# A fifth tile for the running block sums, and another spread of the partner steps, in a decoder layer on one core

## The chip, the core and the metric

The kernel runs on one core of a Trainium2 chip. The metric is the device time of one execution in microseconds; of several runs the median counts. The profile is that of one execution, taken by the hardware profiler. Engine names are those of the profile: PE (matrix multiply) and PEld (its weight loads), DVE (vector), ACT (scalar), POOL and SP; a DMA is issued by an engine's queue (here SP's and POOL's) and carried out by 16 DMA engines, which all queues share. POOL's queue is q0 in the profile, SP's is q1.

## The reference

One decoder layer for 256 tokens of width 2048, all in float32. What matters here is the first, largest part:

```python
h = rmsnorm(x, pre_norm_g[l])
proj = h @ w_in[l]                       # (256, 2048) @ (2048, 18448)
(a_q, a_k, a_v, a_g, a_lr, b_q, b_k, b_v, b_g, m_a, m_b) = jnp.split(proj, offsets, axis=-1)
...
y_a = o_a @ w_branch_a[l]
y_b = o_b @ w_branch_b[l]
merged = jax.nn.sigmoid(m_a) * y_a + jax.nn.sigmoid(m_b) * y_b
x = x + rmsnorm(merged @ w_out[l], post_norm_g[l])
```

Between them stand a gated linear attention (o_a) and a differential attention (o_b).

## The kernel before

**Products in float32.** A weight tile arrives in float32 and is split into two parts: ACT copies it to `hi` (line 361) and DVE subtracts, `lo = r - hi` (line 362). PE then multiplies `hi` with both parts of the input and `lo` with the input's upper part alone. Work is cut in *halves*, a half being a piece of 128 x 1024 weights; `take` hands halves out in the fixed order of the list `seq`, `emit_half` splits them `AHEAD = 3` halves before their use, and each of the tags `hi` and `lo` has 3 buffers. So the split of a half waits until PE is done with the half that stands three before it.

**Sets.** From about 77 to 631 us most columns of `proj` are computed as nine *sets* of 1024 columns (sets 0 to 8, the last one of a quarter of the rows). A set's weights are four blocks B11, B12, B21, B22, the input is cut in four as well, and seven block products stand in place of eight, in the order `PRODUCTS = (1, 3, 5, 6, 2, 7, 4)` (`block_products`). The weights that they take are running sums of blocks:

- the tile `a` is B11 in product 1; B12 is added to it by an accumulating DMA (`accumulate`, line 255), then it serves product 5; DVE adds `b` (line 264), then it serves product 6; DVE adds `c`, then it serves product 4;
- the tile `b` is B22 in product 3; B12 is added by an accumulating DMA, then it serves product 7;
- the tile `c` is B21 in product 2.

Each block has two tiles (t = 0, 1) of 1 MB, and each tile two halves h, so a full set has 14 *slots* (product, t) of two halves. A set half is 6 matmuls of 512 columns. The tiles of `a` and `b` come from one ring, the tag `chain`, with 4 buffers (line 230); a block load into it (line 231) is issued by POOL, from set 1 on, and waits until a buffer is free, that is, until DVE has taken the last `lo` of an older tile. An accumulating DMA waits for the `lo` of product 1 (for `a`) or for the sum by DVE (for `b`), so that nothing still needs the old contents. The tiles of `c` are loaded by SP in four pieces of 512 KB (line 247).

**One bank for four products.** Products 1, 6, 7 and 4 add up in one PSUM bank `x` (line 832). After product 6 and after product 7 DVE reads the bank as it then stands (lines 886 and 895, output `gr`), and the next product that is added to `x` has to come after that read. Product 2 stands between 6 and 7; nothing stands between 7 and 4.

**Partners.** Between the set slots stand halves of other matrices (`others`: first v4, then the q and k of the linear attention, then heads of the differential one). The table `PARTNERED` (line 36) names the slots after which one such *partner* half follows; the set's order is made in `phase_steps`. From set 1 on a partner half is 16 matmuls, 8 of 512 columns and 8 of 256, and needs one split of its own (`raw`). Two partner halves share one 1 MB tile `raw` of three buffers, which SP loads (line 312); a load waits for the second half's `lo` three tiles before. The bank of a partner is its own, so a partner never waits for `x`.

**Order.** A scheduler orders what each engine issues. PE is held to program order in this stretch (`keep_in_program_order`). A DMA, however, may be placed ahead of its place in the program if its buffer is free, and DVE's and ACT's instructions may change places.

Of the kernel before, what the change touches and what calls it, by code (L numbers as in the profile page):

```python
# [6 lines left out]
F32 = mybir.dt.float32  # L7
# [7 lines left out]
P = 128  # L15
# [14 lines left out]
SETS = 8  # L30
# [2 lines left out]
MERGE = (0, 1, 6)  # L33
LEAD = 6
EARLY = (0, 1)
PARTNERED = ((3, 0), (5, 1), (6, 0), (6, 1), (2, 1), (7, 0), (7, 1), (4, 1))
LAST_PARTNERED = (5, 6, 2, 7)
BIG = 18
MORE = 16
# [109 lines left out]
def hybrid_kernel(ctx: ExitStack, tc, xt, xn, preg, postg, w, w2, gkb, glag, lamv, diffg, ident_d, causal_d, lmask_d, out):  # L149
# [10 lines left out]
    blocks = joint.enter_context(tc.tile_pool(name="blocks", bufs=2))  # L160
    pools = [joint.enter_context(tc.tile_pool(name="first", bufs=2))]
    count = [0]
# [56 lines left out]
    chain = {}  # L219
# [7 lines left out]

    def link(s, name, t):
        count[0] += 1
        c = blocks.tile([P, 2048], F32, tag="chain", name=f"{name}_{count[0]}", bufs=4)  # L230
        (pool if s else sp).dma_start(c, block(s, {"a": 0, "b": 3}[name], t))
        chain[s, name, t] = c

    def emit_set(s, prod, t, h):
        c = slice(1024 * h, 1024 * h + 1024)
        few = 1 if s == SETS else 2
        if h == 0 and s < SETS and (prod, t) in ((7, 1), (4, 0)) and (t or s + 1 < SETS):
            link(s + 1, "a", 1 - t)
        if h == 0 and s < SETS and (prod, t) == (4, 1):
            link(s + 1, "b", 0)  # L240
        if h == 0 and prod == 1 and s < SETS and (s == 0 or t == 0):
            link(s, "b", t if s == 0 else 1)
        n = 2 * few * (PRODUCTS.index(prod) - PRODUCTS.index(2)) + 2 * t + h + LEAD
        if 0 <= n < 2 * few:
            i, j = n // 2, n % 2
            raws[s, i, j] = u([P, 1024], "c")
            sp.dma_start(raws[s, i, j], block(s, 2, i)[:, 1024 * j : 1024 * j + 1024])
        a, b = chain[s, "a", t], chain[s, "b", t]
        return raws[s, t, h] if prod == 2 else (b if prod in (3, 7) else a)[:, c]
# [449 lines left out]
    def sum_operands():  # L699
# [5 lines left out]
        temps = []  # L705
        for n in range(2):
            count[0] += 1
            temps.append(blocks.tile([P, 2, 8, P], F32, tag="chain", name=f"temp_{count[0]}", bufs=4))
        r1, s2, s4 = (temps[n // 2][:, n % 2] for n in range(3))

        def part(i, j, q):
# [569 lines left out]
    for g in (2, 3):  # L1281
        parts = other_parts(2 * SETS) if g == 3 else None
        banks = token_major(f"ag{g}", 512, x_ops, LANES)
        t = u2([P, 2, 512], "ua")
# [283 lines left out]
    for g in (2, 3):  # L1568
# [7 lines left out]
        if g == 2:  # L1576
            total(0, 2, bank, 2)
            for b in range(2):
                xres.append([])
                for i in range(2):  # L1580
                    t = u([P, 1024], "xres")
# [3 lines left out]
    t = total(0, 3, bank)  # L1585
# [10 lines left out]
    for c in range(2):  # L1596
# [6 lines left out]
        if c == 0:  # L1603
            t = cell(1, 3)[:, :256]
# [4 lines left out]
        else:  # L1609
            end = ps("bg")  # L1610
            c = slice(TURNED[0] % 1024, TURNED[0] % 1024 + 512)
            t = yg[1, 1][:, c]
# [67 lines left out]
```

## Time and profile before

| what | value |
|---|---|
| median of three runs | 1117.03 us (1115.91 to 3435.76) |
| the profiled execution | 1115.6 us |
| its span, from first to last instruction | 1113.8 us, that is 1.8 us less |
| busy share of PE, DVE, ACT, POOL | 98%, 84%, 66%, 15% |
| granted PE clock over the span | 0.997 |
| read from HBM, written | 264.12 MB, 27.26 MB |

How to read it: the share of PE counts a matmul from its start to its modelled end, and matmuls overlap, so a PE that is shown busy may still be slower than its own pace. The pace is read from the distance between the starts of successive matmuls. A timeline row has the start in us, the length in us, the engine, the line, the operation, out<-in by tile names, the form and the count of instructions merged in the row; what stands in brackets is the engine's idle time before it and who ended it. A row of the table by stretches has the stretch, its length, then per engine the busy time and the count, then the granted PE clock, the mean busy share of the 16 DMA engines and the rate in GB/s.

### The profile page before, as it was taken

The numbers are of one execution on the slowest core, as the hardware profiler recorded it, in microseconds if no ns is written. First come the engines' busy times: TensorE is split into PE (matmuls) and PEld (weight loads), VectorE is DVE, ScalarE is ACT, GpSimd is POOL, SyncE is SP. The second block draws the span as 40 slices with busy tenths as digits, with TensorE's granted clock in tenths as the row PEclk, the third lists the DMA queues.
The fourth block names the chain that finished last, engine by engine and source line by source line (L and its number), as shares of the span: only waits on it lengthen the run. The fifth ranks groups of instructions, "written<-read, shape, count | busy, mean of one in ns | idle before, by whom it ended". The sixth has DMA issues, their size and how long they took to land.

```text
span 1113.8 us, 15403 instructions
## 1 busy us (share of the span) xinstructions
PE 1089.5 (98%) x5416; PEld 918.1 (82%) x5416; DVE 939.8 (84%) x1276; ACT 739.5 (66%) x1068; POOL 164.5 (15%) x245
## 2 busy tenths in 40 slices
PE   9999999999999999999999999999999999999997
PEld 8999877878787787878787888888888888888886
DVE  7888979889797988889798889986878887879896
ACT  7886766657666675666676666555776767566662
POOL 0111121211102121221211210022011011101000
PEclk9999999999999999999999999999999999999999
DMA  9889796887879798888968776679898788988852
GB/s 349 289 290 307 242 331 170 335 192 276 234 220 331 225 302 207 328 203 289 277 189 251 260 271 197 213 283 319 279 295 286 256 306 245 331 285 282 272 180 104
DMA packets 66669, 292.40 MB, mean 263 GB/s; under 512 B 8672, under 2 KB 11744, under 8 KB 49184
## 3 DMA queue, kind: packets, MB, share of 16 engines
q1 hardware_dynamic: 38944, 177.43, 45.3%
q0 software_dynamic: 27072, 113.26, 37.2%
q8 instruction: 42, 0.69, 0.2%
q10 hardware_dynamic: 576, 0.73, 0.2%
q14 instruction: 35, 0.29, 0.1%
HBM read 264.12 MB, written 27.26 MB: 262 GB/s over the span
## 4 chain that ended last, share of the span: by engine, by line
PE 79%; DMA 10%; DVE 6%; issue 3%; ACT 2%; POOL 1%; POOLq 0%; ACTq 0%; SPq 0%; DVEq 0%
PE mm L558 50%; PE bg L558 19%; DMA a<-in_w_dram 9%; DVE lo L362 3%; PE mm L546 2%; PE bg L546 2%; ACT hi L361 1%; DMA raw<-in_w_dram 1%; DVE a L264 1%; PE mm L531 1%; PE bg L986 1%; PE bg L531 1%; PE bg L1153 0%; PE bg L1127 0%; DVE p L882 0%
## 5 line engine op out<-in xcount | busy, mean ns | idle before, releaser
L361 ACT ACTIVATE hi<-raw 128x1024 fp32r<-128x1024 f32 (+3 forms) x237 | 242.7, 1028 | 148.3 <-PE mm L558 65.9
L362 DVE TENSOR_TENSOR lo<-raw,hi 128x1024 fp32r<-128x1024 f32 (+3 forms) x239 | 281.4, 1183 | 42.8 <-ACT hi L361 39.1
L362 DVE TENSOR_TENSOR lo<-a,hi 128x1024 fp32r<-128x1024 f32 x136 | 165.8, 1221 | 55.1 <-ACT hi L361 51.2
L361 ACT ACTIVATE hi<-a 128x1024 fp32r<-128x1024 f32 x136 | 143.9, 1058 | 83.1 <-DMA a<-in_w_dram 30.9
L558 PE MATMUL mm<-hi,xs 128*128 128x512 f32 (+1 forms) x728 | 184.8, 384 | 0.0
L558 PEld LDWEIGHTS mm<-hi,xs 128*128 128x128 f32 x728 | 135.5, 188 | 22.3
L558 PE MATMUL bg<-xs,hi 128*128 128x512 f32 x512 | 132.5, 391 | 0.0
L558 PEld LDWEIGHTS bg<-xs,hi 128*128 128x128 f32 x512 | 96.7, 189 | 19.3
L558 PE MATMUL mm<-lo,xs 128*128 128x512 f32 (+1 forms) x364 | 104.0, 385 | 0.3 <-DVE lo L362 0.3
L362 DVE TENSOR_TENSOR lo<-b,hi 128x1024 fp32r<-128x1024 f32 x68 | 81.3, 1219 | 10.4 <-ACT hi L361 10.4
L361 ACT ACTIVATE hi<-b 128x1024 fp32r<-128x1024 f32 x68 | 71.2, 1058 | 28.5 <-PE mm L558 18.4
L558 PEld LDWEIGHTS mm<-lo,xs 128*128 128x128 f32 x364 | 67.4, 188 | 14.8 <-DVE lo L362 3.2
L558 PEld LDWEIGHTS bg<-xs,lo 128*128 128x128 f32 x512 | 68.7, 190 | 10.9 <-DVE lo L362 7.1
L558 PE MATMUL bg<-xs,lo 128*128 128x256 f32 x512 | 72.9, 285 | 1.6 <-DVE lo L362 1.6
L558 PE MATMUL mm<-xs,hi 128*128 128x512 f32 x256 | 68.0, 397 | 0.0
L255 POOL DMA_DIRECT2D b<-in_w_dram x34 | 29.2, 859 | 167.4 <-DVE a L264 124.5
L558 PEld LDWEIGHTS mm<-xs,hi 128*128 128x128 f32 x256 | 46.2, 189 | 7.8
L558 PE MATMUL mm<-hi,oah 128*128 128x512 f32 x128 | 50.8, 397 | 0.0
L558 PE MATMUL mm<-hi,oal 128*128 128x512 f32 x128 | 50.0, 391 | 0.0
L361 ACT ACTIVATE hi<-c 128x1024 fp32r<-128x1024 f32 x34 | 36.0, 1060 | 13.9 <-PE mm L558 10.6
L264 DVE TENSOR_TENSOR a<-a,b 128x1024 f32<-128x1024 f32 x34 | 41.5, 1220 | 0.3
L362 DVE TENSOR_TENSOR lo<-c,hi 128x1024 fp32r<-128x1024 f32 x34 | 41.1, 1216 | 0.0
(419 smaller groups left out, 2180.0 us busy)
## 6 DMA issues: line engine op xcount, KB each, us to landing
raw<-in_w_dram SPq DMA_DIRECT2D x102, 1024.0 KB, 7.1
c<-in_w_dram SPq DMA_DIRECT2D x34, 512.0 KB, 9.1
a<-in_w_dram POOLq DMA_DIRECT2D x34, 512.0 KB, 12.4
b<-in_w_dram POOLq DMA_DIRECT2D x34, 512.0 KB, 7.9
a<-in_w_dram POOLq DMA_DIRECT2D x15, 1024.0 KB, 6.5
b<-in_w_dram POOLq DMA_DIRECT2D x15, 1024.0 KB, 10.5
raw<-in_w_dram SPq DMA_DIRECT2D x14, 832.0 KB, 6.9
gr<-gr POOLq DMA_DIRECT2D x9, 512.0 KB, 4.2
```

The costliest lines, as they stand in the source:

```text
L255: pool.dma_start(chain[s, name, i][:, c], block(s, 1, i)[:, c], accum_op=ALU.add)
L264: dve.tensor_tensor(out=a, in0=a, in1=chain[s, "b", i][:, c] if second else raws[s, i, h], op=ALU.add)
L361: act.activation(hi_t[:, a:b], r[:, a:b], AF.Copy)
L362: dve.tensor_tensor(out=lo_t[:, a:b], in0=r[:, a:b], in1=f32(hi_t[:, a:b]), op=ALU.subtract)
L531: i = pe.matmul(out, lhs, rhs, start=first and n == 0, stop=last and n == len(pairs) - 1, **kw)
L546: i = pe.matmul(banks[g][b][:, :n], a[part][:, P * b : P * b + P], w[:, n * g : n * g + n], start=first, stop=last)
L558: i = pe.matmul(*args, **kw)
L986: pe.matmul(o, xk[:, P * c : P * c + P], xq.rearrange("p (b c t) -> p b c t", b=2, c=4)[:, :, c, :], start=i == 0, stop=i == 1)
```

## The change

```diff
-PARTNERED = ((3, 0), (5, 1), (6, 0), (6, 1), (2, 1), (7, 0), (7, 1), (4, 1))
+PARTNERED = ((1, 1), (3, 1), (5, 1), (6, 0), (6, 1), (2, 1), (7, 0), (4, 0))
...
     def link(s, name, t):
         count[0] += 1
-        c = blocks.tile([P, 2048], F32, tag="chain", name=f"{name}_{count[0]}", bufs=4)
+        c = blocks.tile([P, 2048], F32, tag="chain", name=f"{name}_{count[0]}", bufs=5)
...
-        if h == 0 and s < SETS and (prod, t) in ((7, 1), (4, 0)) and (t or s + 1 < SETS):
-            link(s + 1, "a", 1 - t)
-        if h == 0 and s < SETS and (prod, t) == (4, 1):
-            link(s + 1, "b", 0)
-        if h == 0 and prod == 1 and s < SETS and (s == 0 or t == 0):
-            link(s, "b", t if s == 0 else 1)
+        name, i = {(7, 0): ("a", 0), (7, 1): ("a", 1), (4, 0): ("b", 0), (4, 1): ("b", 1)}.get((prod, t), (None, 0))
+        if h == 0 and s < SETS and name and (i == 0 or s + 1 < SETS):
+            link(s + 1, name, i)
+        if h == 0 and s == 0 and prod == 1:
+            link(s, "b", t)
...
-            temps.append(blocks.tile([P, 2, 8, P], F32, tag="chain", name=f"temp_{count[0]}", bufs=4))
+            temps.append(blocks.tile([P, 2, 8, P], F32, tag="chain", name=f"temp_{count[0]}", bufs=5))
```

The tag `chain` has 5 buffers instead of 4 (1 MB more). In the program the four block loads of the next set stand at the slots (7, 0), (7, 1), (4, 0) and (4, 1), where they stood at (7, 1), (4, 0), (4, 1) and the next set's (1, 0). Of a set's eight partners three change place: (3, 0), (7, 1) and (4, 1) lose theirs, and (1, 1), (3, 1) and (4, 0) get one. So two partners instead of one stand between product 1 and product 5. The lines after 228 move up by one in the changed kernel.

On POOL, at the border from set 1 to set 2, `a` and `b` rows of line 231 are block loads (1 MB) and rows of line 255 (254 after the change) accumulating DMAs (512 KB each); `gr` and `gl` are results that are written out. Before:

```order
L231 DMA a_1896<-in_w_dram 128x2048
L231 DMA a_1942<-in_w_dram 128x2048
L183 DMA gr_1966<-gr_1798 128x1024
L231 DMA b_1969<-in_w_dram 128x2048
L231 DMA b_2011<-in_w_dram 128x2048
L255 DMA a_1896<-in_w_dram 128x1024 x2
L183 DMA gl_2036<-gl_1872 128x1024
L255 DMA a_1942<-in_w_dram 128x1024 x2
```

With the change, at the same place (`a_1872` is the first tile of set 2, `a_2388` that of set 3):

```order
L231 DMA a_1922<-in_w_dram 128x2048
L231 DMA b_1945<-in_w_dram 128x2048
L231 DMA b_1991<-in_w_dram 128x2048
L183 DMA gr_1989<-gr_1825 128x1024
L231 DMA a_2388<-in_w_dram 128x2048
L254 DMA a_1872<-in_w_dram 128x1024 x2
L254 DMA a_1922<-in_w_dram 128x1024
L183 DMA gl_2059<-gl_1898 128x1024
L254 DMA a_1922<-in_w_dram 128x1024
```

There are four block loads ahead of the accumulating DMAs in both. What moved is which: the first `a` of a set is now loaded a whole set early, as the fourth of the row, and the other three stand one place further up.

On PE, the border from product 7 to product 4 of set 1 (`r3h` and `r3l` are the input of product 7, `xs` that of product 4; `mm_1543` is the bank `x`; `bg` rows are a partner). Before:

```order
L558 MATMUL mm_1543<-lo_1911,r3h 128x512 x2
L558 MATMUL bg_1968<-xs_75,hi_1920 128x512 x2
L558 MATMUL bg_1968<-xs_76,hi_1920 128x512 x2
L558 MATMUL bg_1968<-xs_77,hi_1920 128x512 x2
L558 MATMUL bg_1968<-xs_78,hi_1920 128x512 x2
L558 MATMUL bg_1968<-xs_75,lo_1921 128x256 x2
L558 MATMUL bg_1968<-xs_76,lo_1921 128x256 x2
L558 MATMUL bg_1968<-xs_77,lo_1921 128x256 x2
L558 MATMUL bg_1968<-xs_78,lo_1921 128x256 x2
L558 MATMUL mm_1543<-hi_1944,xs_79 128x512 x4
```

With the change:

```order
L557 MATMUL mm_1543<-hi_1934,r3h 128x512
L557 MATMUL mm_1543<-hi_1934,r3l 128x512
L557 MATMUL mm_1543<-lo_1935,r3h 128x512 x2
L557 MATMUL mm_1543<-hi_1947,xs_79 128x512 x4
L557 MATMUL mm_1543<-lo_1948,xs_79 128x512 x2
L557 MATMUL mm_1543<-hi_1967,xs_80 128x512 x4
L557 MATMUL mm_1543<-lo_1968,xs_80 128x512 x2
L557 MATMUL bg_1944<-xs_79,hi_1977 128x512 x2
```

The partner that stood between the last matmul of product 7 and the first of product 4 now follows product 4's first slot. On DVE, the same border, where line 895 (894) is the read of the bank. Before:

```order
L362 TENSOR_TENSOR lo_1921<-raw_1908,hi_1920 128x1024
L805 TENSOR_TENSOR q_1874<-bg_1875,q_1874 128x2x128
L362 TENSOR_TENSOR lo_1945<-a_1376,hi_1944 128x1024
L895 TENSOR_TENSOR gr_1798<-mm_1543,p_135_1710 128x512
L362 TENSOR_TENSOR lo_1955<-a_1376,hi_1954 128x1024
```

With the change:

```order
L361 TENSOR_TENSOR lo_1925<-b_1472,hi_1924 128x1024
L361 TENSOR_TENSOR lo_1935<-b_1472,hi_1934 128x1024
L361 TENSOR_TENSOR lo_1948<-a_1351,hi_1947 128x1024
L361 TENSOR_TENSOR lo_1968<-a_1351,hi_1967 128x1024
L894 TENSOR_TENSOR gr_1825<-mm_1543,p_135_1733 128x512
```

The read of the bank stood behind one `lo` of product 4's first slot and stands behind both now. It is so in sets 0 to 7; set 8 keeps a partner after product 7.

## The prediction

> **What bounds the kernel now.** First the head of the profile's page and its chain of work that ended last, by engine.
>
> ```profile
> span 1113.8 us, 15403 instructions
> PE 79%; DMA 10%; DVE 6%; issue 3%; ACT 2%; POOL 1%; POOLq 0%; ACTq 0%; SPq 0%; DVEq 0%
> ```
>
> PE holds 79% of the chain, but 10% of it are DMAs. So I looked for the places where PE waits for one. The groups of PE by line, with buffer numbers left out, have the idle time before them in their last field:
>
> ```profile
> L558 PE MATMUL mm<-hi,r1h 128*128 128x512 f32 x68 | 28.5, 420 | 12.5 <-ACT hi L361 12.5
> L558 PE MATMUL mm<-hi,s4h 128*128 128x512 f32 x68 | 26.8, 394 | 0.4 <-ACT hi L361 0.4
> ```
>
> `r1h` is the input of product 5: its matmuls stand 12.5 us idle, those of product 3 (`s4h`) 0.4. Idle time counts from the modelled end of a matmul, so it is too small. The true loss is the time from the first to the last matmul of product 5 less its own pace. The pace, and the end of product 7 of set 1 with the partner behind it, on PE's timeline:
>
> ```profile
> 200.46 0.40 PE L558 MATMUL mm<-hi,r3h 128*128 128x512 f32 x1
> ...
> 202.75 0.62 PE L558 MATMUL mm<-lo,r3h 128*128 128x512 f32 x2
> 203.20 1.98 PE L558 MATMUL bg<-xs,hi 128*128 128x512 f32 x8
> 205.01 1.11 PE L558 MATMUL bg<-xs,lo 128*128 128x256 f32 x8
> 205.96 1.09 PE L558 MATMUL mm<-hi,xs 128*128 128x512 f32 x4
> ```
>
> From 200.46 to 203.20 are 12 matmuls: 2.74 us, 0.228 each, so a set half takes 1.37; the partner half takes 205.96 - 203.20 = 2.76. Product 5 has 24 matmuls, 5.47 us. The table by stretches gives its windows in sets 1 to 7 (first number after the stretch: its length):
>
> ```profile
> 164.21:171.79 7.58, 6.59 (x25) 1.00 0.71 140
> 228.00:236.63 8.63, 6.57 (x26) 1.00 0.83 165
> 292.41:301.05 8.64, 6.58 (x26) 1.00 0.82 162
> 357.59:366.40 8.81, 6.61 (x26) 1.00 0.80 159
> 422.17:429.99 7.82, 6.02 (x26) 1.00 0.79 174
> 486.27:494.05 7.78, 6.04 (x25) 1.00 0.76 165
> 550.33:559.46 9.13, 7.29 (x26) 0.85 0.63 133
> sum 58.39, PE 45.70; mean PE 6.53
> ```
>
> 58.39 - 7 x 5.47 = 20.1 us are lost there: 2.1, 3.2, 3.2, 3.3 in sets 1 to 4 (11.8) and 2.4, 2.3, 3.7 in sets 5 to 7 (8.3). What is late is the last accumulating DMA into `a`. POOL's and ACT's timelines of set 2:
>
> ```profile
> 212.44 0.89 POOL L255 DMA_DIRECT2D a<-in_w_dram  x1 [1.92 <-DVE lo L362]
> ...
> 218.49 0.85 POOL L255 DMA_DIRECT2D a<-in_w_dram  x1 [0.61 <-DVE lo L362]
> 233.69 1.06 ACT L361 ACTIVATE hi<-a 128x1024 fp32r<-128x1024 f32 x1 [1.47 <-DMA a<-in_w_dram]
> ```
>
> Asked for at 218.49, it lands at about 233.6, 15.1 us later, and PE waits for the copy that ACT makes of it, until 234.75. Why it takes so long, the stretches of all engines say (last two fields: DMA share, GB/s):
>
> ```profile
> 188.00:198.00 10.00, 10.00 (x48) 7.97 (x47) 10.00 (x11) 7.29 (x8) 1.12 (x2) 1.00 0.22 88
> 198.00:222.00 24.00, 24.00 (x118) 20.17 (x117) 18.97 (x19) 16.18 (x20) 6.18 (x9) 1.00 1.00 380
> 222.00:234.00 12.00, 10.54 (x49) 8.12 (x47) 7.96 (x7) 5.38 (x6) 0.86 (x1) 1.00 1.06 235
> ```
>
> The DMA engines idle before 198 (share 0.22), are full until 222 with block, `c` and `raw` loads, and only then serve the accumulating DMAs. These wait for bytes, not for their issue.
>
> **The change part by part.** *Fifth tile.* In POOL's order four block loads still stand ahead of the accumulates, so no bytes leave the queue ahead of them. What comes a slot sooner are the blocks of products 1 and 3. Product 3 waits 0.4 us by its group, 1.0 us in pace (all of it in set 1, whose blocks are late): credit 1.0.
>
> *Partners.* Without a partner behind (7, 1), the split that frees a `raw` tile, and with it SP's queue, comes one slot and partner sooner, 2 x 1.37 + 2.76 = 5.5 us. SP's rows now:
>
> ```profile
> 198.71 0.33 SPq L312 DMA_DIRECT2D raw<-in_w_dram  x1
> 199.09 2.42 SPq L247 DMA_DIRECT2D c<-in_w_dram  x4
> ```
>
> They would be asked for near 193, in the idle stretch. Of 3 MB (8.3 us at 380 GB/s) some 4 us of transfer then lie before 198, and the full stretch ends near 218. Against it, the next `raw` load is asked for at (3, 1), about 225, beside the last accumulate. What that costs is seen in product 3's two accumulates, the first alone, the second with a `raw` load asked for 0.6 us behind it (POOL's and SP's timelines, and the issue rows with the us to landing of the two, in the same order):
>
> ```profile
> 229.09 0.86 POOL L255 DMA_DIRECT2D b<-in_w_dram  x1 [9.75 <-DVE a L264]
> 237.68 0.85 POOL L255 DMA_DIRECT2D b<-in_w_dram  x1 [7.73 <-DVE a L264]
> 238.30 0.33 SPq L312 DMA_DIRECT2D raw<-in_w_dram  x1
> b<-in_w_dram POOLq DMA_DIRECT2D x1, 512.0 KB, 7.0
> b<-in_w_dram POOLq DMA_DIRECT2D x1, 512.0 KB, 8.9
> ```
>
> So 1.9 us go back: net the last accumulate lands 2 us sooner (bounds: 4.0 if nothing goes back, 0 if the sooner loads only fill the queue). The Trainium skill's page "DMA: Bandwidth & Descriptors" (section "Queues, rings and completion order") says that each DMA engine takes the queues that have work in turn, a packet at a time. By an estimate from it the `raw` load would halve the accumulate's rate, 2.5 us in place of 1.9, and the sum below would be 0.6 x 7 = 4 us higher; the rows 7.0 and 8.9 are nearer to the smaller price, and I keep it.
>
> In sets 5 to 7 another thing delays the last accumulate, two result writes ahead of it on POOL:
>
> ```profile
> 414.49 0.57 POOL L183 DMA_DIRECT2D dl<-dq  x1 [1.07 <-DVE dq L783]
> 415.05 0.94 POOL L255 DMA_DIRECT2D a<-in_w_dram  x1
> ```
>
> The change does not move these writes, and there the `c` loads come to stand behind the next `raw`, so the gain is smaller: between none and the 2 us of the other sets, and nearer to none, 0.5 us.
>
> *The bank.* Product 4 adds to the bank that DVE reads after product 7. DVE's timeline at that place in set 1:
>
> ```profile
> 201.75 1.23 DVE L362 TENSOR_TENSOR lo<-raw,hi 128x1024 fp32r<-128x1024 f32 x1 [0.80 <-ACT hi L361]
> 202.89 0.42 DVE L805 TENSOR_TENSOR q<-bg,q 128x256 f32<-128x256 f32 x1
> 203.23 1.22 DVE L362 TENSOR_TENSOR lo<-a,hi 128x1024 fp32r<-128x1024 f32 x1
> 204.36 0.69 DVE L895 TENSOR_TENSOR gr<-mm,p 128x512 f32<-128x512 f32 x1
> ```
>
> The read ran at 204.36 to 205.05, and the partner (203.20 to 205.96) hid it. Now nothing stands between, and DVE's order has both `lo` of (4, 0) ahead of the read. Put on the same clock: the last matmul of product 7 ends at 203.37; DVE takes the first `lo` at 201.75, the second at 202.95 (pitch 1.2), the read from 204.1 to 204.8; PE goes on at about 204.85 instead of 203.20. Price 1.6 us. Floor 1.0: end of product 7 to the read at once, 0.17 + 0.1 + 0.69. Ceiling 2.8: one more DVE operation of 1.2 in front. I take 1.6, because the rows give DVE 0.80 us idle ahead of its `lo` there: it is not behind. It comes in sets 0 to 7: 8 x 1.6 = 12.8 us (8.0 to 22.4). Queued behind the wait on PE are both slots of product 4 and the next set; PE waits for nothing else meanwhile, the splits of (4, 0) being done, so nothing of it is hidden. But the accumulates, which wait for bytes, gain these 1.6 us on PE.
>
> *Product 5 with both.* Sets 1 to 4: the last accumulate comes 2.0 us sooner and PE 1.6 later, 3.6 together, against losses of 2.1 to 3.3: gone but for about 0.2 a set of scatter. Sets 5 to 7: 0.5 + 1.6 = 2.1 against 2.4, 2.3 and 3.7, mean 2.8: 0.7 a set stays. Credit 20.1 - 4 x 0.2 - 3 x 0.7 = 17.2. The other moves (three partners elsewhere, the same matmuls) cost nothing: PE does the same work, and DVE and ACT have at least as long between splits.
>
> Sum on the profiled execution: its span of 1113.8 and 1.8 around it are 1115.6; 1115.6 - 1.0 - 17.2 + 12.8 = 1110.2. The median of the runs shown, 1117.03, is 1.4 higher, and the fastest of them is 1115.91; I forecast **1110**.
>
> **The clock.** In set 7 a wait was followed by slow matmuls (PE's timeline, then the stretch; the granted clock is its third number from the end):
>
> ```profile
> 556.73 0.80 PE L558 MATMUL mm<-hi,r1h 128*128 128x512 f32 x1 [1.77 <-ACT hi L361]
> 554.50:560.00 5.50, 3.73 (x10) 2.65 (x10) 3.29 (x3) 3.76 (x4) 0.40 (x1) 0.71 0.24 46
> ```
>
> The other windows of product 5 show a clock of 1.00 with stalls of much the same size, so it happened once in seven: (1 - 0.71) x 5.5 = 1.6 us. If every bank wait did so, 8 x 1.6 = 13 us came on top. The Trainium skill ("TensorE: Matmul & The Clock Gate", section "What's actually happening") lets the clock fall only after an idle window of about 3.4 us; the fall after 1.77 us in this trace speaks against counting on that, though by it the sum stays at 1110.
>
> **The rivals.**
>
> *Replaced, not removed (about 1116).* The sooner loads only fill the queue and the last accumulate lands as late as before; then product 5 gains only the 1.6 us by which PE itself is later: 7 x 1.6 = 11.2 and 1.0 against 12.8, 1115.6 + 0.6 = 1116 (1115 to 1118). For it: POOL's order, with as many loads ahead as before, and the `raw` load put beside the last accumulate. Against it: the idle stretch from 188 to 198, into which 3 MB are moved.
>
> *Cheap bank wait (about 1102).* DVE reads at the floor, 8 x 1.0 = 8.0, and all losses at product 5, the residuals too, go: 1115.6 - 21.1 + 8.0 = 1102.5 (1099 to 1105). For it: DVE's 0.80 us idle. Against it: the order of DVE, two `lo` ahead of the read.
>
> *Slower: DVE late at the bank (about 1126).* If ahead of the read stands one more operation, the wait is 2.8 us: 8 x 2.8 = 22.4; with a credit of no more than 7 x 1.6 + 1.0 = 12.2, the time is 1125.8 (1119 to 1133, the upper end with some slow-clock matmuls). The point from which it decides: a bank wait above 18.2 / 8 = 2.3 us eats the whole credit. For it: DVE is 84% busy, and in 188 to 198 it was busy for 10.00 of 10 us. Against it: the 0.80 us idle at 201.75.
>
> *It does not do what it says.* That the `raw` and `c` loads are not asked for sooner, because SP stands behind something else: about 1126 again, counted with that case.
>
> **How the numbers follow.** The forecast (1104 to 1115) has 0.47; replaced 0.20; cheap bank wait 0.17; slower 0.14; anything else 0.02. The predicted time is the forecast's 1110. The range leaves out half of the slower case and the lower third of the cheap one, about 0.15: 1100 to 1121. A change of 2%, 22 us, is about what a measurement of this kernel tells from none: the bounds are 1094.7 and 1139.4. The cheap case barely reaches the lower (0.03) and the slower case the upper (0.02), so 0.95 within.
>
> **What would show it.** Right: the windows of product 5 near 5.7 us in sets 1 to 4 and 6.2 in sets 5 to 7; `raw` and `c` asked for some 5 us sooner against PE, with a DMA share well above 0.22 in the ten us before product 7 ends; a new idle time of some 1.6 us on PE before the first matmul of product 4 (input `xs`), its releaser DVE's `gr` at line 894, in eight sets. Wrong: a set's period that stays at 64 us and more with the wait merely in another place; a wait at product 4 over 2.3 us or under 1.0; losses at product 5 above 1 us in sets 1 to 4; a granted clock under 1.00 behind the waits.

## The result, and the profile after

The changed kernel took 1101.96 us (median of 4 runs, 1100.74 to 1104.04), the kernel before in the same comparison 1116.47 us: a ratio of 0.9878, 95% interval 0.9853 to 0.9904. That is 14.5 us less by the medians, where 7 was forecast: right in direction and inside the range, but twice the gain. (One of the four runs of the kernel before took 3435.76 us, for a reason that is not known; it is left out of the ratio, though not of the median.) The profiled execution took 1102.76 us, 12.8 less than that of before; all terms below are set against these 12.8.

The head and the chain of the page after:

```profile
span 1101.0 us, 15367 instructions
PE 89%; DMA 3%; DVE 3%; issue 2%; ACT 2%; POOL 1%; POOLq 0%; SPq 0%; ACTq 0%; DVEq 0%
```

DMAs fell from 10% of the chain to 3%, and PE rose from 79% to 89%. The groups of PE say where the old wait went and where a new one is (last field: idle time before them, and who ended it):

```profile
L557 PE MATMUL mm<-hi,xs 128*128 128x512 f32 (+1 forms) x728 | 185.4, 385 | 10.4 <-DVE gr L894 10.4
L557 PE MATMUL mm<-hi,r1h 128*128 128x512 f32 x68 | 27.5, 404 | 2.6 <-ACT hi L360 2.6
```

Product 5 (`r1h`) waits 2.6 us in place of 12.5, and these 2.6 lie in set 8. The 10.4 us of the first group (`xs` is the input of products 1, 2 and 4) are product 4's wait for DVE's read of the bank. The windows of product 5 in sets 1 to 7:

```profile
166.74:171.97 5.23, 5.23 (x24) 1.00 0.94 204
228.73:233.96 5.23, 5.23 (x24) 1.00 0.97 239
290.72:295.96 5.24, 5.24 (x25) 1.00 0.93 216
352.72:357.96 5.24, 5.24 (x25) 1.00 0.96 204
414.72:419.97 5.25, 5.25 (x24) 1.00 1.03 284
476.84:482.55 5.71, 5.65 (x25) 1.00 1.04 274
539.50:544.73 5.23, 5.23 (x24) 1.00 1.05 291
sum 37.13, PE 37.07; mean PE 5.30
```

They run from the first start to the last start of product 5, which is 23 steps of 0.228, or 5.24: six of seven run at PE's own pace, with 0.5 us lost in set 6. The windows of before, 58.39 in sum, reach one step further, to the end of product 5; from first to last start they are 56.6. Why, SP's rows and the stretches around them tell:

```profile
191.31 0.33 SPq L311 DMA_DIRECT2D raw<-in_w_dram  x1
191.69 2.22 SPq L246 DMA_DIRECT2D c<-in_w_dram  x4
182.00:192.00 10.00, 10.00 (x50) 8.42 (x49) 10.00 (x12) 7.80 (x9) 0.56 (x1) 1.00 0.52 172
192.00:216.00 24.00, 22.71 (x112) 18.93 (x111) 19.36 (x20) 16.15 (x19) 5.51 (x9) 1.00 0.98 366
216.00:228.00 12.00, 12.00 (x60) 10.14 (x59) 9.72 (x9) 7.93 (x8) 1.27 (x2) 1.00 1.06 248
```

The `c` loads are asked for at 191.69, 37.0 us before product 5 of set 2 starts (228.73). Before it was 199.09, 28.9 us ahead of 228.00. The stretch of some 10 us ahead of the full one has a DMA share of 0.52 in place of 0.22. The last accumulate, on POOL, its us to landing, and ACT's copy of what it brought:

```profile
216.17 1.10 POOL L254 DMA_DIRECT2D a<-in_w_dram  x1
a<-in_w_dram POOLq DMA_DIRECT2D x1, 512.0 KB, 14.7
230.93 1.06 ACT L360 ACTIVATE hi<-a 128x1024 fp32r<-128x1024 f32 x1 [0.67 <-DMA a<-in_w_dram]
```

It lands 2.1 us after the start of product 5 (before: 5.6), the copy ends at 232.0, and PE takes it at 232.8 without a wait. And the bank, on the timelines of PE and DVE in set 1:

```profile
203.93 1.16 PE L557 MATMUL mm<-hi,xs 128*128 128x512 f32 x4 [1.29 <-DVE gr L894]
201.96 1.22 DVE L361 TENSOR_TENSOR lo<-a,hi 128x1024 fp32r<-128x1024 f32 x1 [0.66 <-ACT hi L360]
203.10 0.68 DVE L894 TENSOR_TENSOR gr<-mm,p 128x512 f32<-128x512 f32 x1
```

The read stands behind the second `lo` and runs from 203.10 to 203.78; with the 0.1 to 0.2 us that every restart costs, PE loses 1.53 us there in each of seven sets and 1.58 in set 0, 12.3 us.

For the whole set phase I took, from the trace, the distance of successive matmul starts less the pace (0.226 us for 512 columns, 0.141 for 256 and the partner's own for others) wherever it was over by more than 0.06. The losses by the input of the matmul that came late, in us:

| loss on PE, sets 0 to 8 | before | after |
|---|---|---|
| product 5, sets 1 to 7 | 19.9 | 0.5 |
| product 3 | 1.4 | 0 |
| product 2, and the partners behind products 5, 6 and 7 (DVE's splits late; 0.5 of it at the slow clock of set 7) | 6.8 | 0 |
| product 4 for the bank | 0 | 12.3 |
| set 8, with the slow clock behind its waits | 2.1 | 6.3 |
| sum | 30.2 | 19.1 |

The other 1.7 of 12.8 us are gaps below 0.06 and what lies outside the sets.

### The profile page after: what moved, and what is told of

Its sections match the earlier page's. It is cut to its first block, busy times and chain, and to the rows that moved or that the text cites. A ratio compares the mean times of both kernels' runs of the same rounds, so it can differ in the third digit from the quotient of the medians.

```text
span 1101.0 us, 15367 instructions
## 1 busy us (share of the span) xinstructions
PE 1079.9 (98%) x5416; PEld 922.2 (84%) x5416; DVE 939.6 (85%) x1276; ACT 742.8 (67%) x1068; POOL 164.7 (15%) x245
## 4 chain that ended last, share of the span: by engine, by line
PE 89%; DMA 3%; DVE 3%; issue 2%; ACT 2%; POOL 1%; POOLq 0%; SPq 0%; ACTq 0%; DVEq 0%
PE mm L557 57%; PE bg L557 22%; DVE lo L361 2%; DMA a<-in_w_dram 2%; PE mm L545 2%; PE bg L545 2%; ACT hi L360 1%; DMA raw<-in_w_dram 1%; PE mm L530 1%; PE bg L985 1%; PE bg L530 1%; PE bg L1152 0%; DVE gr L894 0%; PE bg L1126 0%; PE bg L1127 0%
## 5 line engine op out<-in xcount | busy, mean ns | idle before, releaser
L557 PE MATMUL mm<-hi,xs 128*128 128x512 f32 (+1 forms) x728 | 185.4, 385 | 10.4 <-DVE gr L894 10.4
L557 PEld LDWEIGHTS mm<-hi,xs 128*128 128x128 f32 x728 | 134.8, 188 | 35.4 <-ACT hi L360 13.5
L360 ACT ACTIVATE hi<-b 128x1024 fp32r<-128x1024 f32 x68 | 72.1, 1060 | 19.9 <-PE mm L557 14.4
L557 PEld LDWEIGHTS mm<-lo,xs 128*128 128x128 f32 x364 | 68.2, 188 | 12.2
L263 DVE TENSOR_TENSOR a<-a,c 128x1024 f32<-128x1024 f32 x34 | 41.1, 1215 | 0.0
```

What stands on the lines that cost most here:

```text
L263: dve.tensor_tensor(out=a, in0=a, in1=chain[s, "b", i][:, c] if second else raws[s, i, h], op=ALU.add)
L360: act.activation(hi_t[:, a:b], r[:, a:b], AF.Copy)
L557: i = pe.matmul(*args, **kw)
```

## The experiments

Times are medians; a ratio is to the kernel before in the same comparison, with its 95% interval. A kernel is named after its edit. "Lost" is counted as in the table above.

**The two halves of the change alone.** `tile_only` is the changed kernel with

```diff
-PARTNERED = ((1, 1), (3, 1), (5, 1), (6, 0), (6, 1), (2, 1), (7, 0), (4, 0))
+PARTNERED = ((3, 0), (5, 1), (6, 0), (6, 1), (2, 1), (7, 0), (7, 1), (4, 1))
```

> The changed kernel with the old spread of the partners: what is left of the change is the fifth tile and the sooner places of the block loads. Theory 1 (the slack of product 5 comes from the second partner between products 1 and 5 and from the wait at the bank, not from the tile): product 5 stalls as before, 16 to 20 us over sets 1 to 7, no wait at the bank, only the wait at product 3 of set 1 (1.0 us) goes: 1113 to 1117 us. Theory 2 (the sooner block loads empty the queue for the accumulating DMAs): at least half of the stall of product 5 goes, 1104 to 1108 us.

`partners_only` is the kernel before with the opposite edit.

> The kernel before with the new spread of the partners, 4 tiles and the old places of the block loads. Theory 1 (second partner and bank wait give the slack): the stalls of product 5 go as in the changed kernel, the bank wait of 1.5 us comes 8 times, 1101 to 1106 us. Theory 2 (the tile gives it): product 5 goes on to stall for 8 us or more in sets 1 to 7, the bank wait comes on top, 1110 to 1122 us.

Measured: `tile_only` 1115.13 us, 0.9989 (0.9974 to 1.0004); `partners_only` 1101.63 us, 0.9865 (0.9841 to 0.9889). The groups of product 5, of `tile_only` first:

```profile
L557 PE MATMUL mm<-hi,r1h 128*128 128x512 f32 x68 | 28.0, 412 | 12.2 <-ACT hi L360 12.2
```

```profile
L558 PE MATMUL mm<-hi,r1h 128*128 128x512 f32 x68 | 26.9, 396 | 2.8 <-ACT hi L361 2.8
```

12.2 us of idle time with the tile alone, 2.8 with the partners alone. The fifth tile and the new places of the block loads bring nothing that can be measured; the table of partners makes the whole gain.

**The bank covered again.** `cover` is the changed kernel with

```diff
-PARTNERED = (... (2, 1), (7, 0), (4, 0))
+PARTNERED = (... (2, 1), (7, 0), (7, 1))
```

> The changed kernel with the partner of (4, 0) put back to (7, 1), so that it covers DVE's read of the bank; everything else as changed. The bank wait, 8 x 1.5 us, goes in every theory. Theory 1: PE comes to product 5 1.5 us sooner, while the accumulates land at most a little sooner; by their landings in the changed kernel (up to 2.9 us behind the start of product 5, 3.0 allowed) 4 to 6 us of stall come back there: 1092 to 1097 us. Rival (the bank wait was free, since PE would have stood at product 5 for the same time): 1100 to 1103 us.

Measured: 1106.43 us, 0.9914 (0.9878 to 0.9951): above the expectation and above its rival. The bank wait went, but product 5 took as much back:

```profile
L557 PE MATMUL mm<-hi,r1h 128*128 128x512 f32 x68 | 29.0, 426 | 11.8 <-ACT hi L360 11.8
```

By set the trace shows two halves: in sets 1 to 4 only 1.9 us are lost in sum, and the set period is 60.4 to 61.7 us (62.0 in the changed kernel), but in sets 5 to 7 the last accumulate lands 5.5 to 6.3 us after product 5's start, and 14.1 us are lost there, some of them by a slow clock behind the wait. These are the sets with result writes ahead of the last accumulates on POOL.

**The bank wait by itself.** `no_read7` is the changed kernel, in which the operation after product 7 adds a kept tile to itself and does not read the bank, so that half of one result block is not the reference's:

```diff
-dve.tensor_tensor(out=halves["r"][:, 1, :], in0=x, in1=kept[5], op=ALU.add)
+dve.tensor_tensor(out=halves["r"][:, 1, :], in0=kept[5], in1=kept[5], op=ALU.add)
```

> The changed kernel, but what DVE computes after product 7 no longer reads the bank (it adds two other tiles of the same shape in its place), so one result block is wrong and product 4 has nothing to wait for; partners, loads and matmuls are as changed. It tells what the bank wait alone costs. Theory 1: the eight waits of 1.5 us at product 4 go (12.2 us) and PE reaches product 5 1.5 us sooner; in sets 5 to 7, where the last accumulate lands only 0.1 to 0.8 us before its deadline, 3 to 5 us of stall come back: 1092 to 1096 us. Rival (the wait is free, every microsecond of it stands at product 5 without it): 1100 to 1103 us.

Measured: 1103.23 us, 0.9886 (0.9868 to 0.9903), the changed kernel's ratio within the intervals: the rival's case, at the upper end of its range. The group of product 5:

```profile
L557 PE MATMUL mm<-hi,r1h 128*128 128x512 f32 x68 | 28.5, 420 | 11.2 <-ACT hi L360 11.2
```

The 12.3 us at the bank are gone, and 12.6 us more are lost at product 5 (17.9 with set 8, 5.3 in the changed kernel). In the changed kernel the bank wait is real, but it is also the time in which the accumulates land. Taking away that one wait without making the transfers sooner wins nothing.

**One partner between products 1 and 5.** `one_between` moves, against the kernel before, only the partner of (7, 1) behind (4, 0); the tile is kept:

```diff
+PARTNERED = ((3, 0), (5, 1), (6, 0), (6, 1), (2, 1), (7, 0), (4, 0), (4, 1))
```

> The changed kernel with one partner between products 1 and 5, as before: partners at (3, 0), (5, 1), (6, 0), (6, 1), (2, 1), (7, 0), (4, 0), (4, 1). Against the kernel before, only the partner of (7, 1) is moved behind (4, 0), and the tile is kept: the raw and c loads are asked for sooner and the bank wait comes, but the second partner is missing. The theory of the prediction (the sooner loads and the bank wait bring product 5 its time): the stalls of product 5 fall from 20 us to under 5, 1103 to 1109 us. Theory 1 (the second partner does it): product 5 still stalls 7 to 12 us, and the bank wait of 12 us comes on top: 1112 to 1118 us.

Measured: 1119.22 us, 1.0031 (1.0017 to 1.0046): 0.3% slower than before, though no more than 4.8 us are lost at product 5 in sets 1 to 7. So on product 5 the prediction's own theory holds; the time lies above the ranges of both. The groups of products 4 and 5:

```profile
L557 PE MATMUL mm<-hi,xs 128*128 128x512 f32 (+1 forms) x728 | 187.7, 389 | 14.6 <-DVE gr L894 14.6
L557 PE MATMUL mm<-hi,r1h 128*128 128x512 f32 x68 | 27.3, 401 | 2.5 <-ACT hi L360 2.4
```

The bank in set 1 of `one_between`:

```profile
202.12 0.42 DVE L804 TENSOR_TENSOR q<-bg,q 128x256 f32<-128x256 f32 x1
204.42 1.17 PE L557 MATMUL mm<-hi,xs 128*128 128x512 f32 x4 [1.83 <-DVE gr L894]
```

The bank wait costs 2.1 us a set here and not 1.5: on DVE an operation on a partner's result stands between the two `lo` ahead of the read. In sets 5 and 6 the granted clock falls behind the wait, and product 4 loses 3.5 and 3.7 us; in sum it loses 19.6, above the 18.2 from which, by the prediction, the bank eats the whole credit. The waits for DVE's splits behind product 5 (0.4 to 0.5 us at the partner of (6, 0), more behind it) are still there, 6.9 us in sum, as in the kernel before.

**The last accumulate given more time, and four partners from product 7 to product 5.** `three` is `cover` with the partner of (5, 1) at (5, 0); `cover2` is the changed kernel with that of (7, 0) at (7, 1); `both` has both edits:

```diff
+PARTNERED = ((1, 1), (3, 1), (5, 0), (6, 0), (6, 1), (2, 1), (7, 0), (7, 1))   three
+PARTNERED = ((1, 1), (3, 1), (5, 1), (6, 0), (6, 1), (2, 1), (7, 1), (4, 0))   cover2
+PARTNERED = ((1, 1), (3, 1), (5, 0), (6, 0), (6, 1), (2, 1), (7, 1), (4, 0))   both
```

> The kernel with the bank covered by the partner at (7, 1) (1106 us, with 12 us idle at product 5, most of it in sets 5 to 7 before the last half), and the partner of (5, 1) moved ahead of it, to (5, 0): the last accumulate has 2.8 us more, nothing else changes in the queues. Theory (only the last accumulate's landing counts): the idle time at product 5 falls from 11.8 us to under 4, the slow clock behind the long waits goes, 1090 to 1096 us. Rival (product 6 has no cover now for DVE's sum and the splits): a wait of 1 to 2 us before product 6 in each set, 1098 to 1106 us.

> The changed kernel with the partner of (7, 0) moved to (7, 1), that of (4, 0) kept: the bank is covered, and between product 7 and product 5 of the next set stand four partners (three in the changed kernel and in the kernel with the partner of (4, 0) at (7, 1)). Theory (what counts is when the block and c loads are asked for against product 5, so a partner more behind them gives the accumulates 2.8 us more): idle time at product 5 under 4 us, 1088 to 1094 us. Rival (the sums by DVE and the c loads between products 2 and 7 lose their cover, or the queue fills again): new waits at products 7 or 4, or stalls at product 5 as in the other covered kernel, 1098 to 1108 us.

> The two covered kernels in one: partners at (1, 1), (3, 1), (5, 0), (6, 0), (6, 1), (2, 1), (7, 1), (4, 0), so the bank is covered, four partners stand between product 7 and the last slot of product 5, and the last accumulate has 2.8 us more. Theory: the idle time that the two had at product 5 in sets 1 to 7 (2.0 and 0.7 us in sets 6 and 7 of the one) goes, only set 8 stalls (4 us): 1089 to 1092 us. Rival (product 2 waits for DVE's splits as in the kernel with the partner at (5, 0), 0.8 us in four sets): 1092 to 1095 us.

Measured: `three` 1093.61 us, 0.9799 (0.9785 to 0.9814); `cover2` 1094.42 us, 0.9809 (0.9791 to 0.9828), a little above its expectation; `both` 1090.67 us, 0.9775 (0.9762 to 0.9789). The group of product 5 in `both`, and its window in set 2:

```profile
L557 PE MATMUL mm<-hi,r1h 128*128 128x512 f32 x68 | 27.5, 405 | 2.5 <-ACT hi L360 2.5
```

```profile
225.50:230.76 5.26, 5.26 (x27) 1.00 0.97 229
```

The period of a set is 60.4 us from set 1 to set 6, which is 28 set halves of 1.37 and 8 partners of 2.76 with nothing lost. `both` is the fastest kernel of this study, 2.2% below the kernel before; of the 7.6 us that it still loses in the sets, 5.9 are in set 8.

**Set 8.** `last_cover` is the changed kernel with

```diff
-LAST_PARTNERED = (5, 6, 2, 7)
+LAST_PARTNERED = (1, 6, 2, 7)
```

> The changed kernel with the first partner of the last set (set 8) put behind product 1 in place of product 5, so that there, too, a partner stands between products 1 and 5. Theory: product 5 of set 8 waits 6.3 us in the changed kernel (2.0 and 1.2 of idle time and the slow clock behind it) because there is no partner between; the partner of 2.8 us takes the idle time and the slow clock away: 1095 to 1098 us. Rival (PE waits there for a DMA that the queue holds up, whatever stands between, or the wait moves to the next product): 1100 to 1103 us.

`both_last` is `both` with five partners in set 8, of which set 7 gives up one:

```diff
-LAST_PARTNERED = (5, 6, 2, 7)
+LAST_PARTNERED = (1, 5, 6, 2, 7)
-... else (prod, t) in PARTNERED
+... else (prod, t) in PARTNERED and slot != (SETS - 1, 2, 1)
```

> As the kernel with both, and set 8 has a fifth partner, behind its product 1, for which set 7 gives up the one at (2, 1). Behind product 1 the earlier trial took 4 us of wait from product 5 of set 8 but left product 6 without cover for DVE's sum; here product 5's own partner stays. Theory: the 4 us of set 8 go, nothing comes in their place: 4 us less than the kernel with both, 1085 to 1088 us. Rival (the waits of set 8 move on to product 2 or 7, or set 7 pays for its partner): no gain, 1089 to 1093 us.

Measured: `last_cover` 1101.03 us, 0.9861 (0.9837 to 0.9884), no clear gain on the changed kernel; `both_last` 1093.13 us, 0.9795 (0.9782 to 0.9809), slower than `both`. The rival's mechanism was right both times (`both_last` lies 0.1 us above its range). In `last_cover` the wait at product 5 shrinks to 0.92 us, and product 6 (`s2h`) waits in its place:

```profile
596.40 0.50 PE L557 MATMUL mm<-hi,r1h 128*128 128x512 f32 x1 [0.92 <-ACT hi L360]
601.07 0.50 PE L557 MATMUL mm<-hi,s2h 128*128 128x512 f32 x1 [1.30 <-ACT hi L360]
```

The partner that was taken from behind product 5 had covered DVE's sum for product 6. In `both_last` set 8 loses 2.1 us less than in `both`, but set 7, which gave a partner up, loses 1.6 us more at product 7. In a set of single slots a partner that is moved only moves the wait.

**Which two partners share a tile.** All tables above also change which partner is the second of its pair, and so when SP's queue, with the `c` loads in it, comes free. Four kernels shift the pairs by one and leave all partners of sets 1 to 7 in place: set 0 gives up its partner at (2, 1) and set 8 gets a fifth. `parity` does it to `both`, `before_pairs` to the kernel before, `after_pairs` to the changed kernel, `four_one_pairs` to `four_one`, which has one partner between products 1 and 5. `before_pairs7`, in which set 7 gives the partner up, is the control.

```diff
-LAST_PARTNERED = (5, 6, 2, 7)
+LAST_PARTNERED = (1, 5, 6, 2, 7)
-... else (prod, t) in PARTNERED
+... else (prod, t) in PARTNERED and slot != (0, 2, 1)
...
+PARTNERED = ((3, 0), (5, 1), (6, 0), (6, 1), (2, 1), (7, 1), (4, 0), (4, 1))   four_one
```

> As the kernel with both and a fifth partner in set 8, but set 0 gives up its partner at (2, 1) in place of set 7. So in sets 1 to 7 the pairs of partners that share a raw tile change: the raw loads are asked for at (1, 1) and (5, 0), no longer at (3, 1), beside the last accumulate. Theory (a raw load beside the last accumulate delays it by 2 to 4 us): the fourth accumulate takes 2 to 4 us less against the third; the time is as in the kernel before it, 1085 to 1088 us, as product 5 hardly stalls there. Rival (the raw load at (1, 1) stands in the queue ahead of the accumulates and delays all four of them): they land 2 to 3 us later, product 5 stalls, 1088 to 1096 us.

> The changed kernel with partners at (3, 0), (5, 1), (6, 0), (6, 1), (2, 1), (7, 1), (4, 0), (4, 1): the bank covered, four partners between product 7 and product 5 of the next set as in the kernel with the partner of (7, 0) at (7, 1), but only one of them between products 1 and 5. Theory A (what counts is how long before product 5 the c and raw loads are asked for, so the place of the partners within that stretch is of no account): idle time at product 5 under 6 us, 1093 to 1099 us. Theory B (it counts that two partners stand between products 1 and 5, after the accumulates are asked for): product 5 stalls for 10 us and more in sets 1 to 7 and the partner behind product 6 waits for DVE, 1102 to 1110 us.

> The kernel before, with the same table of partners, but set 0 gives up its partner at (2, 1) and set 8 has a fifth behind its product 1: in sets 1 to 7 all partners stand as before, only the pairs that share a raw tile shift by one, so SP's raw loads, and the c loads behind them, are asked for at other places. Theory B (the pairs, and so the time of the c and raw loads against product 5, make the gain): c asked for some 35 us before product 5, the stalls of product 5 fall from 20 us to under 8, no bank wait: 1098 to 1105 us. Theory A (a second partner between products 1 and 5 makes it): stalls as before, 1112 to 1118 us.

> Control for the kernel before with shifted pairs: set 8 has the fifth partner too, but set 7 gives up its one at (2, 1), so the pairs of sets 1 to 6 stay as before. Both theories: product 5 stalls as before in sets 1 to 6, the time is that of the kernel before within what set 8 and set 7 change, 1110 to 1119 us. If it is below 1106 us, the fifth partner in set 8 makes the gain and not the pairs.

> The kernel with one partner between products 1 and 5 and four between product 7 and product 5 (1114.4 us, c asked for 25 to 27 us before product 5), with the pairs shifted by one as in the other kernel (set 0 gives up (2, 1), set 8 has a fifth). Theory B: the c loads are asked for some 35 us before product 5, its stalls fall under 5 us in sets 1 to 7, 1092 to 1098 us. Theory A: with only one partner between, product 5 goes on to stall 8 us and more, 1105 to 1115 us.

> The changed kernel with the pairs shifted the other way (set 0 gives up (2, 1), set 8 has a fifth): the partners of sets 1 to 7 stand as changed, two between products 1 and 5, the bank wait stays, but the c loads are asked for later, some 28 us before product 5. Theory B: product 5 (or product 2, by DVE's late splits) stalls again, 10 us and more in sets 1 to 4: 1108 to 1118 us. Theory A: as changed, 1098 to 1103 us.

Measured: `parity` 1105.63 us, 0.9911 (0.9896 to 0.9927), against 1093.13 of `both_last`; `before_pairs` 1133.13, 1.0148 (1.0124 to 1.0172), against 1116.52, 1.0009 (0.9997 to 1.0021) of its control; `after_pairs` 1116.90, 1.0002 (0.9992 to 1.0013), against 1101.96; `four_one_pairs` 1131.52, 1.0134 (1.0113 to 1.0154), against 1114.41, 0.9989 (0.9973 to 1.0004) of `four_one`. The expectations named the wrong direction for `before_pairs` and `four_one_pairs` (I took the shift to bring the `c` loads sooner; it brings them later) and the right one for `after_pairs`. For `parity` the rival named the direction, but both its ranges lie 10 us and more below the time; `four_one`, too, lies above both of its ranges. SP's rows of `before_pairs` at the border of sets 1 and 2, and its product 5:

```profile
202.82 2.26 SPq L247 DMA_DIRECT2D c<-in_w_dram  x4
L558 PE MATMUL mm<-hi,r1h 128*128 128x512 f32 x68 | 30.4, 447 | 23.7 <-ACT hi L361 23.7
```

The same of `after_pairs`, with the bank:

```profile
197.95 2.24 SPq L246 DMA_DIRECT2D c<-in_w_dram  x4
L557 PE MATMUL mm<-hi,xs 128*128 128x512 f32 (+1 forms) x728 | 189.1, 391 | 13.7 <-DVE gr L894 13.7
L557 PE MATMUL mm<-hi,r1h 128*128 128x512 f32 x68 | 27.5, 405 | 4.9 <-ACT hi L360 4.9
```

And of `parity`, where the late splits by DVE hit product 6 (`s2h`):

```profile
201.49 2.22 SPq L246 DMA_DIRECT2D c<-in_w_dram  x4
L557 PE MATMUL mm<-lo,s2h 128*128 128x512 f32 x68 | 22.2, 408 | 7.0 <-DVE lo L361 7.0
```

Ten of the kernels side by side, for set 2, by the time that the first `c` load is asked for ahead of product 5's first matmul and the time that the last accumulate lands behind it. The last accumulate may land at 3.0: three set halves of 1.37 stand in product 5 ahead of the half that needs it, less ACT's copy of 1.06. The losses are all those of PE in sets 1 to 4, at product 5 and elsewhere.

| kernel | partners between products 1 and 5 | c asked, us ahead | last accumulate lands, us behind | lost in sets 1 to 4 | median us |
|---|---|---|---|---|---|
| changed | 2 | 37.0 | 2.1 | 6.1 | 1101.96 |
| both | 2 | 35.5 | 1.6 | 0.0 | 1090.67 |
| cover2 | 2 | 35.4 | 2.2 | 0.1 | 1094.42 |
| one_between | 1 | 30.9 | 4.0 | 16.3 | 1119.22 |
| after_pairs | 2 | 30.9 | 4.0 | 17.4 | 1116.90 |
| before | 1 | 28.9 | 5.6 | 16.5 | 1116.47 |
| parity | 2 | 27.2 | 6.5 | 14.5 | 1105.63 |
| four_one | 1 | 26.9 | 6.1 | 19.8 | 1114.41 |
| before_pairs | 1 | 25.3 | 7.8 | 27.5 | 1133.13 |
| four_one_pairs | 1 | 22.4 | 8.3 | 29.9 | 1131.52 |

In set 2 the later the `c` loads are asked for, the later the last accumulate lands, but for two pairs of rows that differ by 0.4 and 0.5 us. The one pair of rows with the same `c` time lands at the same time whether one or two partners stand between products 1 and 5 (`one_between` and `after_pairs`, both 30.9 and 4.0), though `after_pairs` asks for that accumulate 3.2 us sooner against product 5. So in sets 1 to 4 it is the queue that decides, as the prediction had it, and not the second partner, as I took it to be in between (theory 1 in the expectations above). The rule is a rough one: in `no_read7` the `c` loads are asked for 34.4 to 35.5 us ahead in sets 1 to 4, and the last accumulate lands anywhere from 0.4 to 6.3 behind.

In sets 5 to 7 the rule does not hold. Before, the `c` loads are asked for 43.7 us ahead of product 5 there and the last accumulate lands 4.8 to 5.2 behind its start; with the change they are asked for later, 35.9 to 37.5 ahead, and it lands sooner, 2.2 to 2.9 behind. Two things differ there. PE comes later by the bank wait: in `no_read7`, without it, the landings are 3.7 to 5.6 behind. And the request for the last accumulate itself comes sooner: before at 415.05 in set 5 (the prediction shows the row), 7.1 us ahead of product 5, with the change 11.5 us ahead of 414.72:

```profile
403.22 1.27 POOL L254 DMA_DIRECT2D a<-in_w_dram  x1
```

Where the cost of a later queue falls differs, too. Over sets 1 to 7 `before_pairs` and `four_one_pairs` lose 16.8 and 18.5 us more at product 5 than `before_pairs7` and `four_one`. `after_pairs` loses only 4.2 more there than the changed kernel and 9.7 more at product 4, by the longer bank wait and the slow clock behind it, and `parity` loses 9.0 at product 6.

A share of the second partner in the time beyond that is not shown. `after_pairs` is 2 us faster than `one_between`, but loses 1.2 us more in sets 1 to 4; `parity` is 9 us faster than `four_one` (5.3 in sets 1 to 4 and 5.6 in sets 5 to 7, less what set 8 takes back), but its partner in product 5 stands at (5, 0) and not at (5, 1).

## Why the prediction was half right

- *Product 5 bounds, by the last accumulate, by the queue.* Right for sets 1 to 4. The kernels of the pairs show it: with no partner of sets 1 to 7 moved, a shift of the `c` loads by 3.5 to 8 us costs 12 to 17 us, in the two that start from one partner between products 1 and 5 all of it at product 5.
- *Fifth tile: 1.0 us.* Nothing measurable came of the tile in the time. The wait at product 3 did go, 1.4 us in two sets, with the tile alone as well as with the partners alone.
- *The loads sooner by 5.5 us, the last accumulate 2.0 sooner and PE 1.6 later, 3.6 together.* The loads came 8.1 us sooner against product 5 in set 2 (37.0 and 28.9), and 6 to 8 us later in sets 5 to 7. The reason that I gave was incomplete: the partner behind (7, 1) is gone, but the pairs shift too. The landing moved by 3.5 us in set 2 (5.6 and 2.1): right. That the next `raw` load stands beside the last accumulate was right as well: it was asked for 3.4 us ahead of product 5, and the last accumulate landed 5.5 us behind the third.
- *Residual of 0.2 in sets 1 to 4 and 0.7 in sets 5 to 7, 2.9 us.* 0.5 us remained. The landings of sets 5 to 7 moved by 1.9 to 3.0 us (forecast 2.1), but what had to move was only the 1.8 us by which 4.8 was over the 3.0 allowed; the rest of each loss was the slow restart behind the wait, which goes with it. 2.4 us more gain. That the bank wait is most of the move is borne out by `no_read7`: without it the landings of these sets are 3.7 to 5.6 behind.
- *The bank: 1.6 us, eight times, 12.8.* It was 1.53 and 12.3. The place, the releaser and DVE's order were as told. The Trainium skill's page on the clock, "TensorE: Matmul & The Clock Gate" (section "What's actually happening"), lets no gap this short lower the clock, and here it did not fall: the granted clock is 1.00 behind all eight waits. Behind the bank waits of `one_between`, with 1.83 us of idle time in place of 1.29, it did fall in two of eight sets, which the page's figure does not foresee.
- *"The other moves [...] cost nothing: PE does the same work, and DVE and ACT have at least as long between splits."* This step failed. It put at nothing what the moved partners do to DVE, and looked for PE's waits at products 3, 4 and 5 alone. In the kernel before, PE also waits for DVE behind product 5. DVE's and PE's timelines, set 2:

```profile
232.25 1.23 DVE L362 TENSOR_TENSOR lo<-a,hi 128x1024 fp32r<-128x1024 f32 x1 [2.49 <-ACT hi L361]
234.78 1.22 DVE L362 TENSOR_TENSOR lo<-a,hi 128x1024 fp32r<-128x1024 f32 x1 [1.30 <-ACT hi L361]
...
243.33 1.22 DVE L362 TENSOR_TENSOR lo<-raw,hi 128x1024 fp32r<-128x1024 f32 x1
244.60 1.22 PE L558 MATMUL bg<-xs,lo 128*128 128x256 f32 x8 [0.26 <-DVE lo L362]
```

  DVE works through from 234.78 to 244.55 without a gap, and the partner behind product 6 waits for the last of these splits; product 2 loses time behind it. Together with product 3 these waits were 8.2 us in the sets; 1.0 of them had been credited. With the change all of them are gone.

  A backlog that the late accumulate leaves on DVE, which stands idle for it, looks like the cause. The runs speak against that as the whole of it. In sets 5 and 6 of `one_between` product 5 loses nothing, and DVE's late splits still cost 1.1 us in each, as in the kernel before. In set 1 of `no_read7`, which has the new table, product 5 loses 3.9 us at full clock, and DVE's late splits 0.2:

```profile
172.48 1.23 DVE L361 TENSOR_TENSOR lo<-a,hi 128x1024 fp32r<-128x1024 f32 x1 [4.43 <-ACT hi L360]
...
180.24 1.22 DVE L361 TENSOR_TENSOR lo<-raw,hi 128x1024 fp32r<-128x1024 f32 x1
```

  From the end of the last split of product 5 to the end of the split for the partner behind product 6 are 7.8 us here, and 8.6 in the kernel before (236.00 to 244.55). DVE's order differs: before, one of the four sums `a<-a,b` stands ahead of that last split of product 5 and three behind it; with the new table two stand ahead and two behind. Behind product 6 and at product 2, the five kernels with (3, 0) and (5, 1) in the table and unshifted pairs lose 4.8 to 5.7 us in sets 0 to 7, and the six with (1, 1), (3, 1) and (5, 1) and unshifted pairs at most 0.4. So the moves of the partners gained 6.8 us through DVE where they were put at nothing. That this one sum is the reason is argued and not shown, as no run moves it alone; and `parity` shows that a late landing (6.5) can cost time at product 6 as well.
- *Set 8 left out of the sum.* It has no partner between its products 1 and 5, and its split runs without the cover of the partner that stood ahead of it at (4, 1). With set 8 itself as before, the kernels that have a partner at (4, 1) lose 2.0 to 2.4 us there, and those without one 3.9 to 6.3. The changed kernel lost 6.3 us in place of 2.1, more than half of the growth by a slow clock behind the wait:

```profile
592.45 0.50 PE L557 MATMUL mm<-hi,r1h 128*128 128x512 f32 x1 [1.82 <-ACT hi L360]
595.53 0.80 PE L557 MATMUL mm<-hi,r1h 128*128 128x512 f32 x1 [0.80 <-ACT hi L360]
595.00:601.00 6.00, 5.47 (x13) 4.33 (x14) 5.49 (x6) 4.03 (x5) 2.32 (x4) 0.52 0.56 105
```

The sum again, with what was measured: product 3 1.4, product 5 19.4, DVE's late splits 6.8, less 12.3 for the bank and 4.2 for set 8, makes 11.1, and 1.7 outside, 12.8; the forecast had 1.0 + 17.2 - 12.8 = 5.4. The 7.4 us between them are 6.8 for DVE's late splits, 2.2 more at product 5, 0.9 at product 3 and the bank and 1.7 outside, less 4.2 in set 8. The rival with the cheap bank wait named nearly the right time (1102), but by luck: the wait was not at its floor of 1.0.

What stays open: why `cover` loses its gain in sets 5 to 7 (result writes stand ahead of the accumulates on POOL there, but so they do in the changed kernel, and no run takes them away), what besides the `c` loads sets the landing in those sets, and whether DVE's order alone accounts for its late splits.

## What to carry to other kernels

A move that leaves PE's work the same is not free of effect: it can change the order of work on the engine that feeds PE, and that shows as small waits two or three steps on. Add up these small waits before putting a move at nothing. Where transfers are limited by bytes, a step that is moved matters by the requests that are released with it, and by all that stands behind them in the same queue: count for each request how long ahead of its need, or of the next urgent transfer, it is made. Check such a rule in every stage, not in one: here it held in four sets and failed in three. And a new wait may be the time in which the old one ran out: before taking it away, ask what will be late next.

## What the runs showed of the hardware

The clock behind a wait is not told by the length of the wait. In set 5 of `cover` PE waits 3.28 us and then runs at a granted clock of 0.57:

```profile
416.19 0.77 PE L557 MATMUL mm<-hi,r1h 128*128 128x512 f32 x1 [3.28 <-ACT hi L360]
416.00:420.00 4.00, 3.81 (x10) 3.03 (x11) 3.83 (x5) 3.57 (x5) 0.00 (x0) 0.57 0.54 107
```

In set 1 of `no_read7` it waits as long, and the clock stays at 1.00:

```profile
172.50 0.50 PE L557 MATMUL mm<-hi,r1h 128*128 128x512 f32 x1 [3.25 <-ACT hi L360]
172.50:176.50 4.00, 3.95 (x17) 3.00 (x18) 4.00 (x5) 3.42 (x5) 0.00 (x0) 1.00 0.38 74
```

In set 8 of the changed kernel it fell behind a wait of 1.82 us and stayed low past one of 0.80. The bank waits of `one_between` have the same idle time, 1.83 us, in every set; these are the stretches behind those of sets 4 and 5:

```profile
398.71:402.71 4.00, 4.00 (x18) 1.00 0.94 334
462.57:466.57 4.00, 4.00 (x11) 0.62 0.96 354
```

Of the 15 bank waits of 1.83 us in `one_between` and `after_pairs` the clock fell behind six, and behind none of the eight of about 1.3 us in the changed kernel. So in these runs a wait of 1.8 to 3.3 us may cost some 2 us more, or nothing.
